# Gate and up of a feed-forward layer as a 2x2 block product: seven products for eight on a quarter of k

## The chip, the cores and the metric

The kernel runs on one core of one Trainium2 chip. The engines are TensorE (PE, with its weight loads as PEld), VectorE (DVE), ScalarE (ACT), GpSimd (POOL) and SyncE (SP, whose queue issues most DMA transfers). The metric is the device time in microseconds, as the median of several runs.

## The reference

One layer on 256 tokens of width 2048, all in float32. The part that the change touches is the feed-forward block, which stands in the layer twice, ahead of the mixer and behind it:

```
def swiglu(h, w_gate, w_up, w_down):
    return (jax.nn.silu(h @ w_gate) * (h @ w_up)) @ w_down

x = x + 0.5 * swiglu(rms_norm(x, ffn1_norm[i]), ffn1_w_gate[i], ffn1_w_up[i], ffn1_w_down[i])
```

`w_gate` and `w_up` are 2048 x 5632 and `w_down` is 5632 x 2048. Between the two feed-forward blocks stand an input projection, a state-space mixer with a GLU, a stick-breaking attention and an output projection; behind the second stands a gated per-layer embedding.

## The kernel before, in words

**Precision.** Every float32 operand of a large product is cut into a high part, rounded to the matmul's format (`hi`), and the rest (`lo`). A product of two such operands is made of three: hi·hi, lo·hi (activation lo, weight hi) and hi·lo. For weights, `split` (L165) does the cut: ScalarE casts `raw` to `whi` (L168), VectorE subtracts to make `wlo` (L171). `whi` and `wlo` have four buffers each, `raw` has three.

**Tiles.** k goes in tiles of 128, in quarters of 512 (one DMA of 1 MB on SP's queue, L274, one `raw`) and in halves of a quarter (2 k tiles, 128 x 1024 numbers, one split). A block of output columns is 512 wide, `NB`. The 256 tokens are two tiles `t` of 128. The activations are stationary, the weights stream: `gemm_half` (L277) sends for one half eight matmuls with `hi` weights (L284 and L285: activation hi, activation lo, for two k tiles and two t) and then four with `lo` weights (L289), into one PSUM bank for each t. `gemm_block` (L291) does this for all halves of k and calls `step()` after each.

**The layer's loop.** `ffn` (L379) is called twice: layer 1 with `bg=s5_prep` (the mixer's preparation runs beside it until block 6), layer 2 without. Each has 11 blocks of columns, `for f in range(NF)`: gate's block over 16 k tiles, its silu on ScalarE (L410), up's block over 16 k tiles, and the product of both on VectorE (L430), from PSUM:

```
hh[:, t * NB : (t + 1) * NB], in0=pu[t], scalar=xn.rs(t), in1=sg[...]
```

`turned` then turns the result on VectorE (L203, into `mid`) and through 16 small DMAs on SP's queue to `hT`, which the down projection cuts into `hhi` and `hlo` (`act`, L436) and multiplies by `w_down`.

**Buffers.** PSUM has four banks of 512 columns for products (`acc`). Activations in halves lie in the tags `nhi`/`nlo` (four buffers each) and `hhi`/`hlo` (two each). Layer 1's normalized input takes all of `n`, and `h` is free until the down projection; layer 2's (`kinds="hhnn"`) takes `h` and two of `n`.

**What sets the order.** The code traces instructions in the order in which it is written, with work put off by a number of steps: `put_off(n, fn)` runs `fn` at the (n+1)th `step()` from there, and a generator given to `start` advances one `yield` at each step. From the trace a list planner issues each engine's queue: it takes what its own costs say is ready, earlier code first, and only instructions in `pin(...)` keep their place. Each engine then works through its queue in that order and waits at semaphores.

Of the kernel before, what the change touches and what calls it, by code (L numbers as in the profile page):

```python
# [9 lines left out]
F32 = mybir.dt.float32  # L10
# [6 lines left out]
P = 128  # L17
# [16 lines left out]
def layer_kernel(ctx: ExitStack, tc: tile.TileContext, a: dict, shapes: dict, out: bass.AP):  # L34
# [45 lines left out]
    def acc(s="acc"):  # L80
        return accp.tile([P, NB], F32, tag="acc", name=uid(s))
# [83 lines left out]
    def split(hi, lo, src, scale=None, pinned=False):  # L165

        if scale is None:
            copy = nc.scalar.copy(hi, src)  # L168
            if pinned:
                pin(copy)  # L170
            nc.vector.tensor_tensor(out=lo, in0=src, in1=hi.bitcast(F32), op=ALU.subtract)  # L171
        else:
            split_each(hi.unsqueeze(1), lo.unsqueeze(1), src.unsqueeze(1), [scale])
# [103 lines left out]
    def gemm_half(ps, half, ts, start, stop, cols=slice(0, NB)):  # L277

        (ahi, alo), (h, hi, lo) = half
        for j in range(2):  # L280
            for t in ts:
                lh = ahi[:, 2 * h + j, t * P : (t + 1) * P]
                ll = alo[:, 2 * h + j, t * P : (t + 1) * P]
                nc.tensor.matmul(ps[t], lhsT=lh, rhs=hi[:, j, cols], start=start and j == 0, stop=False)  # L284
                nc.tensor.matmul(ps[t], lhsT=ll, rhs=hi[:, j, cols], start=False, stop=False)  # L285
        for j in range(2):
            for t in ts:
                lh = ahi[:, 2 * h + j, t * P : (t + 1) * P]
                nc.tensor.matmul(ps[t], lhsT=lh, rhs=lo[:, j, cols], start=False, stop=stop and j == 1)  # L289

    def gemm_block(act, w, n0, nkt, first=()):  # L291

        ps = [acc(), acc()]
        for k0 in range(0, nkt, 4):
            part = act(k0 // 4)
            quarter = first[k0 // 4] if k0 // 4 < len(first) else weight_halves(w, k0, min(4, nkt - k0), n0)
            for half in list(quarter):
                k = k0 + 2 * half[0]
                gemm_half(ps, (part, half), range(TT), k == 0, k + 2 == nkt)
                if first and half[0] == 0 and k0 + 4 < nkt:  # L300
                    act(k0 // 4 + 1)
                step()
        return ps
# [75 lines left out]
    def ffn(i, xn, nxt, bg=None):  # L379
        wg, wu, wd = (a[f"ffn{i}_w_{s}"][0] for s in ("gate", "up", "down"))  # L380
        hT = []
        pools = ExitStack()
        early = 6 if bg else NF
        hp = pools.enter_context(phase(f"h{i}"))
        side = ExitStack()
        prep = bg(side) if bg else None
        mids = {}

        def turned(hp, f, hh):
            pair, n_pair = f // 2, min(2, NF - f // 2 * 2) * 4  # L390
            if f % 2 == 0:
                mids[pair] = com("mid")[:, : 128 * TT * n_pair].rearrange(
                    "p (q t b f) -> p q t b f", q=4, t=TT, b=32
                )
            for t in range(TT):
                turn_blocks(mids[pair], hh[:, t * NB : (t + 1) * NB], t, f % 2 * 4, 4)
            if f % 2 or f == NF - 1:
                hf = get(hp, f"hT{pair}", T * n_pair)
                turn_quarters(hf.rearrange("p (t s f) -> p t s f", t=TT, f=n_pair), mids[pair], 8)
                hT.append(hf.rearrange("p (s f) -> p f s", f=n_pair))  # L400

        for f in range(NF):
            if prep and f == min(early, NF - 1):
                finish(prep)
                side.close()
                prep = None
                hp = pools.enter_context(phase(f"h{i}b"))
            def gate():
                for t in range(TT):
                    nc.scalar.activation(sg[:, t * NB : (t + 1) * NB], pg[t], AF.Silu, scale=xn.rs(t))  # L410

            first = ()
            if f == 0 and bg:
                warm_up(10)
                first = first_quarters(wg, xn)
            pg = gemm_block(xn, wg, f * NB, KD, first)
            sg = com("sg")
            if f == 0 and bg:
                for n in range(ND):
                    put_off(n, load_x, n)  # L420
                    put_off(n + 2, xn.squares, n)
                put_off(6, gate)
            else:
                gate()
            pu = gemm_block(xn, wu, f * NB, KD)
            if prep and f == 0:
                start(prep)
            hh = com("h")
            for t in range(TT):
                nc.vector.scalar_tensor_tensor(  # L430
                    out=hh[:, t * NB : (t + 1) * NB], in0=pu[t], scalar=xn.rs(t),
                    in1=sg[:, t * NB : (t + 1) * NB], op0=ALU.mult, op1=ALU.mult,
                )
            put_off(2, turned, hp, f, hh)

        def act(k):  # L436
            hi, lo = halves("h")
            split(hi, lo, hT[k // 2][:, k % 2 * 4 : k % 2 * 4 + 4, :])
            return hi, lo

        for n in range(ND):
            ps = gemm_block(act, wd, n * NB, F // P)
            for t in range(TT):
                nc.vector.scalar_tensor_tensor(
                    out=xt[t][n], in0=ps[t], scalar=0.5, in1=xt[t][n], op0=ALU.mult, op1=ALU.add
                )
            put_off(2, nxt.block, n)
        pools.close()
# [779 lines left out]
```

## Time and profile before

| | before |
|---|---|
| median of 3 runs | 1901.69 us (1900.64 to 1903.12) |
| span of the profiled execution, first to last instruction | 1898.3 us |
| what lies between that span and the median | 3.4 us |
| instructions | 23928 |
| matmuls on TensorE | 9142 |

The page lists for the profiled execution only its span; no other time of this one execution is given. "Busy" counts time in which an engine has an instruction running; matmuls overlap, so a matmul's mean duration (392 ns) is longer than the distance between two. "Idle before" in a group's row is the time that the engine stood still ahead of its instructions, with the instruction that ended the wait. In a timeline the columns are start and duration in us, engine, line, operation, output and input with their shapes, how many were merged, and the wait.

### The profile page before, as it was taken

To read this page: it belongs to the slowest core of one execution; us is meant where nothing else is said; L and a number is where in the kernel's file an instruction comes from. 1 tells how busy PE (TensorE), PEld (TensorE's weight loads), DVE (VectorE), ACT (ScalarE), POOL (GpSimd) and SP (SyncE) were. 2 spreads that over 40 slices of the span, in tenths; PEclk is the share of its full clock that TensorE was granted. 3 is DMA by queue.
4 is the path that set the end of the run, shared out by engine and by line. 5 is a ranking of instruction groups with operands and counts; after the bars stand their busy time and mean duration, and the time that the engine had idled before them with its cause. 6 is when DMAs were issued, how large, how long until landed. Compare 5 with 4: busy or idle time off the path is not lost.

```text
span 1898.3 us, 23928 instructions
## 1 busy us (share of the span) xinstructions
PE 1888.4 (99%) x9142; PEld 1563.8 (82%) x9142; DVE 1299.6 (68%) x1604; ACT 1105.7 (58%) x1217; POOL 30.6 (2%) x48
## 2 busy tenths in 40 slices
PE   9999999999999999999999999999999999999998
PEld 7888888888888888888898888888888888888886
DVE  8996765555688987686567655555555568898855
ACT  7466664444578886455785544444444457888754
POOL 0000000000000000010010000000000000000000
PEclk9999999999999999999999999999999999999999
DMA  8677877666656657776545656665656665666553
GB/s 323 225 243 260 261 247 236 197 209 209 215 185 209 209 190 277 235 243 205 172 156 172 222 187 217 200 210 191 220 189 216 201 223 188 205 209 209 196 200 122
DMA packets 225714, 402.55 MB, mean 212 GB/s; under 512 B 16704, under 2 KB 46656, under 8 KB 225472
## 3 DMA queue, kind: packets, MB, share of 16 engines
q1 hardware_dynamic: 212976, 385.99, 61.2%
q10 hardware_dynamic: 12624, 15.04, 2.3%
q8 instruction: 71, 1.16, 0.3%
q14 instruction: 43, 0.35, 0.1%
HBM read 369.53 MB, written 14.68 MB: 202 GB/s over the span
## 4 chain that ended last, share of the span: by engine, by line
PE 94%; DVE 2%; ACT 1%; issue 1%; DMA 1%; SPq 0%; DVEq 0%; ACTq 0%
PE acc L284 30%; PE acc L285 30%; PE acc L289 30%; DVE hlo L171 1%; ACT hhi L168 1%; DVE wlo L171 1%; DVE nlo L180 1%; PE aux L715 0%; PE acc L994 0%; PE acc L989 0%; PE acc L985 0%; PE aux L634 0%; DMA raw<-in_ffn_w_gate 0%; DMA h<-in_p_turned 0%; PE aux L767 0%
## 5 line engine op out<-in xcount | busy, mean ns | idle before, releaser
L171 DVE TENSOR_TENSOR wlo<-raw,whi 128x1024 fp32r<-128x1024 f32 x666 | 810.5, 1225 | 451.5 <-ACT whi L168 446.9
L168 ACT CAST whi<-raw 128x1024 fp32r<-128x1024 f32 x666 | 697.8, 1054 | 710.1 <-PE acc L285 658.4
L284 PE MATMUL acc<-whi,nhi 128*128 128x512 f32 x1568 | 614.2, 392 | 1.2 <-ACT whi L252 0.7
L285 PE MATMUL acc<-whi,nlo 128*128 128x512 f32 x1568 | 610.6, 389 | 0.0
L289 PE MATMUL acc<-wlo,nhi 128*128 128x512 f32 x1568 | 420.7, 389 | 0.0
L285 PE MATMUL acc<-whi,hlo 128*128 128x512 f32 x1056 | 411.6, 390 | 0.7
L284 PE MATMUL acc<-whi,hhi 128*128 128x512 f32 x1056 | 411.0, 389 | 0.0
L284 PEld LDWEIGHTS acc<-whi,nhi 128*128 128x128 f32 x1568 | 294.3, 188 | 64.9 <-ACT whi L252 1.8
L289 PEld LDWEIGHTS acc<-wlo,nhi 128*128 128x128 f32 x1568 | 294.2, 188 | 61.7 <-DVE wlo L171 0.2
L285 PEld LDWEIGHTS acc<-whi,nlo 128*128 128x128 f32 x1568 | 294.4, 188 | 60.0
L289 PE MATMUL acc<-wlo,hhi 128*128 128x512 f32 x1056 | 282.2, 389 | 0.0
L285 PEld LDWEIGHTS acc<-whi,hlo 128*128 128x128 f32 x1056 | 198.2, 188 | 44.7 <-DVE hlo L171 3.3
L289 PEld LDWEIGHTS acc<-wlo,hhi 128*128 128x128 f32 x1056 | 198.2, 188 | 41.2
L284 PEld LDWEIGHTS acc<-whi,hhi 128*128 128x128 f32 x1056 | 198.2, 188 | 40.7
L171 DVE TENSOR_TENSOR hlo<-hT,hhi 128x1024 fp32r<-128x1024 f32 x88 | 188.4, 2141 | 48.7 <-ACT hhi L168 48.7
L168 ACT CAST hhi<-hT 128x1024 fp32r<-128x1024 f32 x88 | 192.2, 2185 | 1.4 <-DMA raw<-in_ffn_w_gate 1.4
L203 DVE STREAM_TRANSPOSE mid<-h 128x512 f32<-128x512 f32 x44 | 47.0, 1156 | 0.0
L430 DVE SCALAR_TENSOR_TENSOR h<-acc,sm,sg 128x512 f32<-128x512 f32 x44 | 31.0, 745 | 19.4 <-PE acc L289 19.4
L410 ACT ACTIVATE sg<-acc,sm 128x512 f32<-128x512 f32 x44 | 27.7, 681 | 0.4 <-DVE sm L196 0.3
L178 ACT ACTIVATE nhi<-h,gains 128x256 fp32r<-128x256 f32 x40 | 24.0, 662 | 0.2 <-DVE h L1010 0.2
L180 DVE SCALAR_TENSOR_TENSOR nlo<-h,gains,nhi 128x256 fp32r<-128x256 f32 x40 | 23.1, 633 | 0.6 <-ACT nhi L178 0.6
L704 POOL COPY dec<-rho 128x512 f32<-128x512 f32 x8 | 10.6, 1348 | 729.0 <-DVE rt L741 564.5
(242 smaller groups left out, 762.7 us busy)
## 6 DMA issues: line engine op xcount, KB each, us to landing
raw<-in_ffn_w_up SPq DMA_DIRECT2D x88, 1024.0 KB, 5.5
raw<-in_ffn_w_down SPq DMA_DIRECT2D x88, 1024.0 KB, 5.0
raw<-in_ffn_w_gate SPq DMA_DIRECT2D x86, 1024.0 KB, 5.1
raw<-in_w_in SPq DMA_DIRECT2D x32, 1024.0 KB, 5.5
raw<-in_w_out SPq DMA_DIRECT2D x16, 1024.0 KB, 5.2
raw<-in_w_ple_gate SPq DMA_DIRECT2D x16, 1024.0 KB, 5.0
hT<-mid SPq DMA_DIRECT2D x160, 64.0 KB, 4.8
h<-mid SPq DMA_DIRECT2D x128, 32.0 KB, 3.7
```

Source lines behind the costliest of these rows:

```text
L168: copy = nc.scalar.copy(hi, src)
L171: nc.vector.tensor_tensor(out=lo, in0=src, in1=hi.bitcast(F32), op=ALU.subtract)
L178: nc.scalar.activation(hi[:, j, :], src[:, j, :], AF.Copy, scale=scale)
L180: nc.vector.scalar_tensor_tensor(out=lo[:, j, :], in0=src[:, j, :], scalar=scale, in1=hi[:, j, :].bitcast(F32), op0=ALU.mult, op1=ALU.subt ...
L203: nc.vector.transpose(mid[:, :, t, :, k0 : k0 + nk].rearrange("p q b f -> p f q b"), src.rearrange("p (f q b) -> p f q b", f=nk, q=4),)
L284: nc.tensor.matmul(ps[t], lhsT=lh, rhs=hi[:, j, cols], start=start and j == 0, stop=False)
L285: nc.tensor.matmul(ps[t], lhsT=ll, rhs=hi[:, j, cols], start=False, stop=False)
L289: nc.tensor.matmul(ps[t], lhsT=lh, rhs=lo[:, j, cols], start=False, stop=stop and j == 1)
L410: nc.scalar.activation(sg[:, t * NB : (t + 1) * NB], pg[t], AF.Silu, scale=xn.rs(t))
L430: nc.vector.scalar_tensor_tensor(out=hh[:, t * NB : (t + 1) * NB], in0=pu[t], scalar=xn.rs(t), in1=sg[:, t * NB : (t + 1) * NB], op0=ALU.m ...
L704: nc.gpsimd.tensor_copy(dvw[:, i], rho4[:, 8 * q : 8 * q + 8].unsqueeze(2).to_broadcast([P, 8, NC]))
```

## The change

In 14 of the 22 blocks of columns (layer 1: f = 7 to 10; layer 2: f = 1 to 10) the first quarter of k of gate and up is done together. With A the activations, cut into two token tiles (rows) and two halves of the quarter (columns), and B the weights, cut into two halves of k (rows) and gate and up (columns), A·B is a 2x2 product of blocks, and it is made of seven products of blocks, by Winograd's scheme, where it was eight. A product of blocks is 128 tokens by 256 of k by 512 columns: six matmuls (four with hi weights, two with lo). The other three quarters of k go on as before, into the same banks.

What each such block has in it:

- `fetch` loads the quarter of gate (`dg`) and of up (`du`), 1 MB each, for the next block, into tiles with one buffer each, and makes four sums of weights on VectorE (128 x 1024 each: `t1`, `t2`, `t3` in place of `b12`, `t4`). `t1`, `t2`, `t4` and `kept` take the free buffers of `h` (layer 1) or `n` (layer 2): `t1`, `t4` two of `hi`, `t2`, `kept` two of `lo`.
- `quarter_sums`, once for each layer, makes four sums of activation blocks and splits them.
- `pair` runs the seven products, each with a split of its own for its 128 x 1024 weights, made two products ahead. They go into three banks `x`, `a`, `y`; four of the sums are copied out by ScalarE on the way (`o6`, `o7` in `kept`, `o1`, `o5`). VectorE adds these copies to each other later (`sums`, three adds of 512), and at the end to the finished banks: `o1` to gate's second token tile ahead of its silu, `o6` and `o7` to both tiles of up. The last product `hh` then reads SBUF instead of PSUM.
- The steps: after products 1, 3, 5 and 6, and after each half of the other quarters, 16 in a block as before.

```diff
+    def product(ps, a, src, start):
+        (ahi, alo), hi, lo = a, *(wp.tile([P, 2, NB], F32R, tag=s, name=uid(s)) for s in ("whi", "wlo"))
+        split(hi, lo, src)
+        def run():
+            for j in range(2):
+                for i, l in enumerate((ahi, alo)):
+                    nc.tensor.matmul(
+                        ps, lhsT=l[:, j], rhs=hi[:, j], start=start and i + j == 0, stop=False, skip_group_check=True
+                    )
+            for j in range(2):
+                nc.tensor.matmul(ps, lhsT=ahi[:, j], rhs=lo[:, j], start=False, stop=j == 1, skip_group_check=True)
+        return run
...
+        def fetch(f, steps=6):
+            def g():
...
+                for d, w in ((dg, wg), (du, wu)):
+                    nc.sync.dma_start(d, w[:NB, f * NB : (f + 1) * NB].rearrange("(j p) n -> p j n", p=P))
+                b11, b21, b12, b22 = dg[:, :2], dg[:, 2:], du[:, :2], du[:, 2:]
...
+                for _ in range(steps):
+                    yield
+                for o, x, y in ((t1, b12, b11), (t2, b22, t1), (b12, b22, b12), (t4, b21, t2)):
+                    nc.vector.tensor_tensor(out=o, in0=x, in1=y, op=ALU.subtract)
+                    yield
...
+        def pair(f, prefetch):
+            (a11, a12, a22), (s1, s2, s3, s4) = left[0]
+            b11, b21, b22, t1, t2, t3, t4, kept = right.pop(f)
+            x, a, y = acc(), acc(), acc()
+            o6, o7 = kept[:, :NB], kept[:, NB:]
+            o1, o5 = get(hp, "o1", NB), get(hp, "o5", NB)
+            todo = [
+                (x, s2, t2, o6), (a, a11, b11, o1), (y, s1, t1, o5), (x, s3, t3, o7), (a, a12, b21, None),
+                (y, s4, b22, None), (x, a22, t4, None),
+            ]
+            runs = []
+            for i, (ps, l, r, o) in enumerate(todo):
+                while len(runs) < min(i + 3, len(todo)):
+                    n = len(runs)
+                    runs.append(product(*todo[n][:3], todo[n][3] is not None and n != 3))
+                runs[i]()
+                if o is not None:
+                    nc.scalar.copy(o, ps)
+                if i % 2 or i == 6:
+                    step()
+            if prefetch:
+                fetch(f + 1)
+            def sums():
+                nc.vector.tensor_tensor(out=o6, in0=o6, in1=o1, op=ALU.add)
+                nc.vector.tensor_tensor(out=o7, in0=o7, in1=o1, op=ALU.add)
+                nc.vector.tensor_tensor(out=o7, in0=o7, in1=o5, op=ALU.add)
+            put_off(3, sums)
+            rest([a, x], wg, f, ())
+            sg = com("sg")
+            nc.scalar.activation(sg[:, :NB], a, AF.Silu, scale=xn.rs(0))
+            nc.vector.tensor_tensor(out=sg[:, NB:], in0=x, in1=o1, op=ALU.add)
+            nc.scalar.activation(sg[:, NB:], sg[:, NB:], AF.Silu, scale=xn.rs(1))
+            z = acc()
+            rest([y, z], wu, f, (1,))
+            hh = com("h")
+            for ps, o in ((y, o6), (z, o7)):
+                nc.vector.tensor_tensor(out=o, in0=ps, in1=o, op=ALU.add)
+            for t, o in enumerate((o6, o7)):
...
+                    out=hh[:, sl], in0=o, scalar=xn.rs(t), in1=sg[:, sl], op0=ALU.mult, op1=ALU.mult
...
         for f in range(NF):
...
+            if f >= first_pair:
+                pair(f, f + 1 < NF)
+                continue
...
+            if f + 1 == first_pair:
+                left.append(quarter_sums(hp, xn(0)))
+                fetch(f + 1, 3)
             pu = gemm_block(xn, wu, f * NB, KD)
```

`rest` is `gemm_block` without the first quarter; `gemm_half` is given a set of token tiles that start afresh, so that `z` starts there and the other banks go on.

More of the change, by code (lines that the diff above doesn't have):

```diff
@@ L275, in weight_halves, with gemm_half @@
         return weight_split(raw, nk, own)
[L277 removed]
+    def gemm_half(ps, half, ts, start, stop, cols=slice(0, NB), **kw):
         (ahi, alo), (h, hi, lo) = half
+        starts = (ts if start else ()) if isinstance(start, bool) else start
         for j in range(2):
@@ L288, in gemm_half, with quarter_sums @@
                 lh = ahi[:, 2 * h + j, t * P : (t + 1) * P]
-                nc.tensor.matmul(ps[t], lhsT=lh, rhs=lo[:, j, cols], start=False, stop=stop and j == 1)
+                nc.tensor.matmul(ps[t], lhsT=lh, rhs=lo[:, j, cols], start=False, stop=stop and j == 1, **kw)
+    def product(ps, a, src, start):
[10 more added lines that the diff above has]
+        return run
+    def quarter_sums(pool, part):
+        hi, lo = part
+        full, s = (com("h").rearrange("p (j t) -> p j t", t=T), com("h").rearrange("p (i j t) -> p i j t", i=4, j=2))
+        nc.vector.tensor_tensor(out=full, in0=hi.bitcast(F32), in1=lo.bitcast(F32), op=ALU.add)
+        a11, a12, a21 = (full[:, 2 * k : 2 * k + 2, t * P : (t + 1) * P] for t, k in ((0, 0), (0, 1), (1, 0)))
+        a22 = full[:, 2:, P:]
+        for o, x, y, op in (
+            (0, a21, a22, ALU.add), (1, s[:, 0], a11, ALU.subtract), (2, a11, a21, ALU.subtract),
+            (3, a12, s[:, 1], ALU.subtract),
+        ):
+            nc.vector.tensor_tensor(out=s[:, o], in0=x, in1=y, op=op)
+        shi, slo = (pool.tile([P, 4, 2, P], F32R, name=uid(n)) for n in ("shi", "slo"))
+        split(shi, slo, s)
+        quarters = [
+            tuple(u[:, 2 * k : 2 * k + 2, t * P : (t + 1) * P] for u in part) for t, k in ((0, 0), (0, 1), (1, 1))
+        ]
+        return quarters, [(shi[:, i], slo[:, i]) for i in range(4)]
     def gemm_block(act, w, n0, nkt, first=()):
@@ new lines, in rest @@
+        def rest(ps, w, f, starts):
+            for k0 in range(4, KD, 4):
+                part = xn(k0 // 4)
+                for half in list(weight_halves(w, k0, 4, f * NB)):
+                    k = k0 + 2 * half[0]
+                    gemm_half(
+                        ps, (part, half), range(TT), starts if k == 4 else False, k + 2 == KD, skip_group_check=True
+                    )
+                    step()
[8 more added lines that the diff above has]
+                (y, s4, b22, None), (x, a22, t4, None),
+            ]
+            runs = []
[7 more added lines that the diff above has]
+                if i % 2 or i == 6:
+                    step()
+            if prefetch:
[16 more added lines that the diff above has]
+            for t, o in enumerate((o6, o7)):
+                sl = slice(t * NB, (t + 1) * NB)
+                nc.vector.scalar_tensor_tensor(
+                    out=hh[:, sl], in0=o, scalar=xn.rs(t), in1=sg[:, sl], op0=ALU.mult, op1=ALU.mult
+                )
+            put_off(2, turned, hp, f, hh)
```

17 lines of the change are left out of this document (15 added, 2 removed).

## The prediction

> **What bounds the kernel now.** I read the page's busy shares and chain first, then its costliest groups.
>
> ```profile
> span 1898.3 us, 23928 instructions
> PE 1888.4 (99%) x9142; PEld 1563.8 (82%) x9142; DVE 1299.6 (68%) x1604; ACT 1105.7 (58%) x1217; POOL 30.6 (2%) x48
> PE 94%; DVE 2%; ACT 1%; issue 1%; DMA 1%; SPq 0%; DVEq 0%; ACTq 0%
> L171 DVE TENSOR_TENSOR wlo<-raw,whi 128x1024 fp32r<-128x1024 f32 x666 | 810.5, 1225 | 451.5 <-ACT whi L168 446.9
> L168 ACT CAST whi<-raw 128x1024 fp32r<-128x1024 f32 x666 | 697.8, 1054 | 710.1 <-PE acc L285 658.4
> ```
>
> TensorE is busy 99% of the span and is 94% of the chain that ended last. ScalarE's cast mostly waits for a buffer that TensorE holds, VectorE's subtraction mostly for the cast: both run ahead and are held back by their four buffers. A matmul less on TensorE is therefore time gained, as long as the two stay ahead. Next the stretches of the stage that changes, as windows (time, then busy PE, PEld, DVE, ACT, POOL, the granted clock, DMA): one column block of the second feed-forward layer, all eleven but the first of them, and the down projection of the first layer.
>
> ```profile
> 1157.50:1201.00 43.50, 43.50 (x193) 36.02 (x192) 22.79 (x21) 18.05 (x18) 0.00 (x0) 1.00 0.70 217
> 1114.00:1550.00 436.00, 436.00 (x1925) 361.03 (x1924) 233.03 (x205) 184.39 (x182) 0.00 (x0) 1.00 0.64 205
> 543.50:716.00 172.50, 172.12 (x757) 141.50 (x756) 154.98 (x120) 141.40 (x120) 0.00 (x0) 1.00 0.59 200
> ```
>
> TensorE has no gap in ten blocks, at full clock. In the down projection VectorE is busy 154.98 of 172.5 us (90%) and ScalarE 82%, and TensorE still loses only 0.38 us: that is how full the helpers may be. Last, the timeline at the ends of blocks: VectorE's first and last product of gate and up in the second layer, then the seam at 1331 on all engines (the seam in order of time).
>
> ```profile
> 1113.31 1.41 DVE L430 SCALAR_TENSOR_TENSOR h<-acc,sm,sg 128x512 f32<-128x512 f32 x2 [1.09 <-PE acc L289]
> ...
> 1548.51 1.41 DVE L430 SCALAR_TENSOR_TENSOR h<-acc,sm,sg 128x512 f32<-128x512 f32 x2 [1.09 <-PE acc L289]
> ```
> ```profile
> 1328.59 1.23 DVE L171 TENSOR_TENSOR wlo<-raw,whi 128x1024 fp32r<-128x1024 f32 x1 [1.50 <-ACT whi L168]
> ...
> 1330.03 1.07 PE L289 MATMUL acc<-wlo,nhi 128*128 128x512 f32 x4
> 1330.22 1.05 ACT L168 CAST whi<-raw 128x1024 fp32r<-128x1024 f32 x1 [1.67 <-PE acc L285]
> ...
> 1330.91 1.41 DVE L430 SCALAR_TENSOR_TENSOR h<-acc,sm,sg 128x512 f32<-128x512 f32 x2 [1.09 <-PE acc L289]
> 1330.93 0.39 PE L284 MATMUL acc<-whi,hhi 128*128 128x512 f32 x1
> ...
> 1332.23 1.22 DVE L171 TENSOR_TENSOR wlo<-raw,whi 128x1024 fp32r<-128x1024 f32 x1
> ...
> 1333.36 2.16 DVE L203 STREAM_TRANSPOSE mid<-h 128x512 f32<-128x512 f32 x2
> ```
>
> From 1113.31 to 1548.51 are ten blocks: 43.52 us each, and with 192 matmuls in one, **226.7 ns a matmul**. A half (12 matmuls) takes 2.72 us, a product of the new kind (6) 1.36 us, of which its four with hi weights take 0.91. At the seam the cast at 1330.22 starts 0.19 us after the last hi matmuls; it fills the buffer of the half that just left and is the *fourth* half from there. So when block time 0 comes (1330.93), three halves lie ready.
>
> **The change part by part.** *Removed:* of the 48 matmuls on the first quarter of k, 42 are left. 14 blocks x 6 x 226.7 ns = **-19.04 us**. The new order sends all six matmuls of a product into one bank; the last resident block does that already, at the same pace:
>
> ```profile
> 1872.09 0.39 PE L284 MATMUL acc<-whi,nhi 128*128 128x512 f32 x1
> ...
> 1872.99 0.62 PE L289 MATMUL acc<-wlo,nhi 128*128 128x512 f32 x2
> 1873.44 0.39 PE L284 MATMUL acc<-whi,nhi 128*128 128x512 f32 x1
> ```
>
> Six in 1.35 us, so the new order costs nothing. [...]
>
> *Added to VectorE and ScalarE, per block.* Prices:
>
> ```profile
> 566.29 2.35 DVE L171 TENSOR_TENSOR wlo<-raw,whi 128x1024 fp32r<-128x1024 f32 x2
> L818 DVE TENSOR_TENSOR sg<-sg,sm 128x1024 f32<-128x1024 f32 x4 | 4.9, 1226 | 0.1
> L1083 DVE TENSOR_TENSOR e<-h,pg 128x512 f32<-128x512 f32 x7 | 4.5, 683 | 0.0
> L1081 DVE TENSOR_TENSOR h<-acc,sg 128x512 f32<-128x512 f32 x7 | 4.6, 687 | 9.6 <-PE acc L289 9.6
> L1105 DVE SCALAR_TENSOR_TENSOR x<-e,sm,x 128x512 f32<-128x512 f32 x7 | 4.8, 745 | 0.1
> L636 ACT COPY m<-aux 128x1024 f32<-128x1024 f32 x8 | 8.1, 1014 | 11.0 <-DMA scr_m1r<-m 8.8 <-PE aux L634 2.2
> L410 ACT ACTIVATE sg<-acc,sm 128x512 f32<-128x512 f32 x44 | 27.7, 681 | 0.4 <-DVE sm L196 0.3
> ```
>
> Two splits back to back take 2.35, so one costs VectorE 1.13 in a row; two 512-wide products take 1.41 (L430), so 0.66 each. VectorE gets three splits more and four sums of weights (7 x 1.13 = 7.9) and six 512-wide adds (6 x 0.66 = 4.0): 22.79 + 11.9 = 34.7 us of a block of 42.16, 82%. That is under the 90% at which the down projection feeds TensorE. ScalarE gets three casts and four copies out of PSUM, each between half of L636 and L410, say 0.6: 18.05 + 3.2 + 2.4 = 23.7 us, 56%. On average both are hidden behind TensorE. The sums of activations, once per layer (five VectorE operations, one split, under 5 us), and the first sums of weights lie in an ordinary block, where VectorE idles 1.5 us of each 2.72.
>
> *The burst* is what can cost. Seven splits in 9.5 us instead of four in 10.9, and right behind the seam. Time from the first product; products 3 to 6 (counting from 0) want their lo weights at 4.99, 6.35, 7.71, 9.07, the first half after them at 9.52 + 1.81 = 11.33; those of 0 to 2 lie ready. VectorE first closes the old block, four operations now instead of two (y+o6, z+o7 from PSUM, then two products): free at 2.64, the last result out at 2.73. Then the splits end at 3.9, 5.0, 6.1, 7.3, the two transposes (2.16) at 9.3, the next half's split at 10.5: every one 0.8 us early or more. ScalarE: the copy of product 0 into `kept` must wait until the old block's `kept` is free (2.73, since only two buffers are left for the pair t2/kept), and product 3 adds onto the same bank at 4.08, so it waits for that copy. If the copy is next on ScalarE it runs from 2.75 to 3.4; if product 5's cast (startable at 2.47, when product 1's hi matmuls are done) is ahead, from 3.4 to 4.1, some 0.2 us late with the hand-over. Both ends: 0 and 0.5 us per block; below 0 nothing, since no gap is there to close. I take 0.2, because the cast is startable earlier, **+2.8 us**. At the end of layer 1 `kept` also holds one of the down projection's two `lo` buffers until 2.73; that split (2.14 on hlo rows) is then out at some 4.9, wanted at 5.44: 0 to 1 us, I take **+0.3**.
>
> *Moved on SP's queue:* the first quarters (two loads of 1 MB) come behind the products into a single buffer that the splits free at about 7.3, so SP may stand there; the raws of gate's three other quarters are already in by then (three buffers), and the sums use them some 15 us later.
>
> ```profile
> raw<-in_ffn_w_gate SPq DMA_DIRECT2D x86, 1024.0 KB, 5.1
> raw<-in_ffn_w_up SPq DMA_DIRECT2D x88, 1024.0 KB, 5.5
> ```
>
> Two landings of 5.1 and 5.5 one after the other fit, bytes are the same: 0. Uncovered it would be 10.6 less the 8.2 us (three halves) that lie ready, 2.4 us per block.
>
> Sum: -19.04 + 2.8 + 0.3 = -15.9. On the span that is 1882.4; the median of the runs shown lies 3.4 us above the span, which I keep: 1901.7 - 15.9 = **1885.8 us**.
>
> **The rivals.** *A: stalls inside the products take a part.* If the transposes come ahead of product 4's split (before, they follow one split after the product, 1333.36), that split ends at 7.0 instead of 5.0, wanted at 6.35: 0.65 us; with the copy's 0.2 some 0.85 a block, 12 us: 1901.7 - 19.0 + 12 = 1894.7. For it: the order at the seam. Against: the fourth split wasn't startable there, and here it is.
>
> *B: ScalarE's queue keeps the order of the code, and the gain is gone.* There product 3's cast stands behind the copy that waits until 2.73: cast 3.4 to 4.5, lo out at 5.7 for 4.99 (0.7 late), and each later one is copy 0.6 + cast 1.0 against 1.36, some 0.25 late each, three times: 1.4 us a block, 20 us, about 1902. [...] What decides is the order in which the program issues them, and on that the trace has two lines of ScalarE:
>
> ```profile
> 1308.46 1.05 ACT L168 CAST whi<-raw 128x1024 fp32r<-128x1024 f32 x1 [1.67 <-PE acc L285]
> 1309.42 1.26 ACT L410 ACTIVATE sg<-acc,sm 128x512 f32<-128x512 f32 x2
> ```
>
> The cast at 1308.46 belongs to up's fourth half and stands in the code behind the silu; it is issued ahead of it. So casts do pass waiting work.
>
> *C, slower: VectorE's queue closes the old block before it splits for the new one,* as the code has it. Then product 0's lo comes at 2.64 + 1.23 = 3.9, wanted at 0.91: 3.0 us a block, 42 us, 1924. With only one split ahead of the closing the next is late by 1.6 (3.87 for 2.27), 22 us, 1905; with two, 0.24. It decides from fewer than two splits ahead on. Against it: three are ahead now. For it: the closing is twice as long and the splits ahead now need sums that are made in the same queue.
>
> **How the numbers follow.** Forecast (0 to 0.5 us a block; 1882.7 to 1890) 0.62; A (to 1897) 0.17; B 0.08; C 0.11; 0.02 for anything else. The low end is -19.04 with no stall, less 1 us for the spread of the runs. The range 1881.5 to 1898 takes in the forecast and A. A difference of 0.2% (3.8 us) is about what this measurement can tell from none: faster 0.78, same 0.09, slower 0.13.
>
> **What would show it.** After: 9058 matmuls (84 fewer), blocks of 42.2 to 42.7 us between VectorE's closing products; VectorE near 34.7 us in each; idle time of TensorE only ahead of the products' lo matmuls or product 3, with the copies on ScalarE as releaser. Blocks over 43.5 us, or weight loads waiting for wlo in sum over 10 us, would make it wrong; gaps right at the seam mean C, casts behind copies mean B, transposes ahead of product 4's split mean A.

## The result, and the profile after

The changed kernel takes 1886.26 us (median of four runs, 1885.17 to 1887.87), the kernel before beside it 1901.16 (1900.09 to 1903.12): ratio 0.9916, 95% interval 0.9904 to 0.9929. The forecast was 1885.8. The page of the profiled execution (1886.81 us, span 1885.0): its span, the busy shares, the chain that ended last, and two groups.

```profile
span 1885.0 us, 24143 instructions
PE 1874.1 (99%) x9058; PEld 1548.1 (82%) x9058; DVE 1460.9 (78%) x1798; ACT 1174.7 (62%) x1317; POOL 32.5 (2%) x48
PE 86%; DVE 3%; issue 2%; ACT 1%; DMA 1%; SPq 0%; DVEq 0%; ACTq 0%
L300 PE MATMUL acc<-whi,shi 128*128 128x512 f32 x112 | 44.5, 397 | 0.0
L285 PE MATMUL acc<-whi,hhi 128*128 128x512 f32 x896 | 348.8, 389 | 0.0
```

9058 matmuls, 84 fewer, and TensorE is still busy 99% of the span. (Lines have moved: the products are L300 with hi weights and L304 with lo, the ordinary halves L285, L286 and L290, the copies L494, the closing adds and products L515 and L518.) One thing to keep in mind: a hi matmul on `shi` lasts 397 ns (the products' other groups 391 to 395), an ordinary one on `hhi` 389.

The length of a block, from VectorE's closing adds at the end of the second layer's first pair block and of its last, and the ten pair blocks of that layer as a window (busy PE, PEld, DVE, ACT, POOL, clock, DMA):

```profile
1153.46 1.29 DVE L515 TENSOR_TENSOR t<-acc,t 128x512 f32<-128x512 f32 x2 [1.09 <-PE acc L290]
...
1535.06 1.29 DVE L515 TENSOR_TENSOR t<-acc,t 128x512 f32<-128x512 f32 x2 [1.09 <-PE acc L290]
```
```profile
1111.06:1535.06 424.00, 424.00 (x1861) 349.25 (x1860) 336.46 (x327) 232.34 (x253) 0.00 (x0) 1.00 0.64 208
```

(1535.06 - 1153.46) / 9 = **42.40 us**, where it was 43.52: 1.12 us a block, 15.7 in fourteen. TensorE has no gap, at a granted clock of 1.00; VectorE is busy 33.65 us of a block (79%), ScalarE 23.23. But 186 matmuls at 226.7 ns are 42.16 us, so each block is 0.24 us longer than its matmuls account for, although nothing waits. The seam and the products in the timeline; the rows are a selection, in order of time:

```profile
1195.86 1.29 DVE L515 TENSOR_TENSOR t<-acc,t 128x512 f32<-128x512 f32 x2 [1.09 <-PE acc L290]
1195.88 0.40 PE L300 MATMUL acc<-whi,shi 128*128 128x512 f32 x1
1197.07 1.41 DVE L518 SCALAR_TENSOR_TENSOR h<-t,sm,sg 128x512 f32<-128x512 f32 x2
1197.28 0.39 PE L300 MATMUL acc<-whi,hhi 128*128 128x512 f32 x1
1197.97 0.58 ACT L494 COPY t<-acc 128x512 f32<-128x512 f32 x1
1198.39 1.22 DVE L171 TENSOR_TENSOR wlo<-du,whi 128x1024 fp32r<-128x1024 f32 x1
1198.67 0.39 PE L300 MATMUL acc<-whi,shi 128*128 128x512 f32 x1
1200.07 0.40 PE L300 MATMUL acc<-whi,shi 128*128 128x512 f32 x1
1200.77 0.37 SPq L450 DMA_DIRECT2D dg<-in_ffn_w_gate  x1
1201.79 1.22 DVE L171 TENSOR_TENSOR wlo<-t,whi 128x1024 fp32r<-128x1024 f32 x1
1202.93 2.31 DVE L203 STREAM_TRANSPOSE mid<-h 128x512 f32<-128x512 f32 x2
1205.65 0.39 PE L285 MATMUL acc<-whi,hhi 128*128 128x512 f32 x1
```

VectorE closes the old block, makes four splits and only then transposes. ScalarE's copy of product 0 into `kept` (1197.97) is done 1.5 us before product 3 starts (1200.07). No instruction in the products is late. Yet the 42 matmuls from 1195.88 to 1205.65 take 232.4 ns each, at a granted clock of 1.00, and the ordinary ones behind them 226.7 again. 42 x 5.7 ns = 0.24 us: that is all of the difference. It isn't only the four products on `shi` and `slo`, at some 233 ns: product 1, on ordinary activations (1197.28 to 1198.67), takes 231.5 ns a matmul, and products 4 and 6 take 231.3 and 231.5.

Where the span's 13.3 us come from: four pair blocks in layer 1 gave 4.5 and ten in layer 2 gave 11.2; the stretch ahead of the pairs lost 1.9, between the layers 0.4, the end 0.15. The stretch ahead runs the same code in both kernels, but for `quarter_sums` and the first `fetch` in its last block, and that block takes 45.67 us in both. Its end is VectorE's last ordinary product in layer 1, at 325.89 in the trace of before; in two executions of the changed kernel (the second from the experiments below):

```profile
327.77 1.41 DVE L558 SCALAR_TENSOR_TENSOR h<-acc,sm,sg 128x512 f32<-128x512 f32 x2 [1.09 <-PE acc L290]
```
```profile
330.25 1.41 DVE L558 SCALAR_TENSOR_TENSOR h<-acc,sm,sg 128x512 f32<-128x512 f32 x2 [1.09 <-PE acc L290]
```

2.5 us apart in one and the same kernel; over all traces here, the slower staggered kernel's (333.0) apart, the point lies between 325.7 and 331.4. From there to the end the two executions agree within 0.1 us (1557.2). So the 1.9 us are within what this stretch varies by from one execution to the next, and the 2.4 us between the spans of these two come from there. Counted from that point on, the change takes the kernel from 1572.4 to 1557.2 us: 15.2 us.

### The profile page after: what moved, and what is told of

It reads as the page before. It is cut to its first block, busy times and chain, and to the rows that moved or that the text cites. A ratio compares the mean times of both kernels' runs of the same rounds, so it can differ in the third digit from the quotient of the medians.

```text
span 1885.0 us, 24143 instructions
## 1 busy us (share of the span) xinstructions
PE 1874.1 (99%) x9058; PEld 1548.1 (82%) x9058; DVE 1460.9 (78%) x1798; ACT 1174.7 (62%) x1317; POOL 32.5 (2%) x48
## 4 chain that ended last, share of the span: by engine, by line
PE 86%; DVE 3%; issue 2%; ACT 1%; DMA 1%; SPq 0%; DVEq 0%; ACTq 0%
PE acc L285 25%; PE acc L286 25%; PE acc L290 25%; PE acc L300 5%; PE acc L304 2%; DVE wlo L171 1%; DVE hlo L171 1%; ACT hhi L168 1%; DVE nlo L180 1%; DMA ceq<-in_ssm_c_laid 1%; PE aux L843 0%; PE acc L1122 0%; PE acc L1117 0%; PE acc L1113 0%; PE aux L762 0%
## 5 line engine op out<-in xcount | busy, mean ns | idle before, releaser
L168 ACT CAST whi<-raw 128x1024 fp32r<-128x1024 f32 x610 | 638.5, 1054 | 523.8 <-PE acc L286 429.7
L171 DVE TENSOR_TENSOR wlo<-raw,whi 128x1024 fp32r<-128x1024 f32 x610 | 737.9, 1226 | 206.2 <-ACT whi L168 201.9
L285 PE MATMUL acc<-whi,nhi 128*128 128x512 f32 x1504 | 589.4, 392 | 1.4 <-ACT whi L252 1.0
L286 PE MATMUL acc<-whi,nlo 128*128 128x512 f32 x1504 | 585.8, 390 | 0.0
L290 PE MATMUL acc<-wlo,nhi 128*128 128x512 f32 x1504 | 403.8, 389 | 0.8 <-DVE wlo L171 0.8
L286 PE MATMUL acc<-whi,hlo 128*128 128x512 f32 x896 | 349.5, 390 | 0.7
L285 PE MATMUL acc<-whi,hhi 128*128 128x512 f32 x896 | 348.8, 389 | 0.0
L285 PEld LDWEIGHTS acc<-whi,nhi 128*128 128x128 f32 x1504 | 282.4, 188 | 62.9 <-ACT whi L252 1.8
L290 PEld LDWEIGHTS acc<-wlo,nhi 128*128 128x128 f32 x1504 | 282.2, 188 | 60.6 <-DVE wlo L171 1.7
L286 PEld LDWEIGHTS acc<-whi,nlo 128*128 128x128 f32 x1504 | 282.5, 188 | 57.8 <-DVE nlo L253 0.3
L290 PE MATMUL acc<-wlo,hhi 128*128 128x512 f32 x896 | 239.5, 389 | 0.0
L286 PEld LDWEIGHTS acc<-whi,hlo 128*128 128x128 f32 x896 | 168.2, 188 | 39.0 <-DVE hlo L171 3.7
L290 PEld LDWEIGHTS acc<-wlo,hhi 128*128 128x128 f32 x896 | 168.2, 188 | 34.9
L285 PEld LDWEIGHTS acc<-whi,hhi 128*128 128x128 f32 x896 | 168.2, 188 | 34.5
L171 DVE TENSOR_TENSOR wlo<-t,whi 128x1024 fp32r<-128x1024 f32 x42 | 51.4, 1223 | 41.8 <-ACT whi L168 41.8
L168 ACT CAST whi<-t 128x1024 fp32r<-128x1024 f32 x42 | 44.2, 1053 | 46.8 <-PE acc L286 46.8
L171 DVE TENSOR_TENSOR wlo<-dg,whi 128x1024 fp32r<-128x1024 f32 x28 | 34.2, 1223 | 20.2 <-ACT whi L168 20.2
L300 PE MATMUL acc<-whi,shi 128*128 128x512 f32 x112 | 44.5, 397 | 0.0
```

What stands on the lines that cost most here:

```text
L285: nc.tensor.matmul(ps[t], lhsT=lh, rhs=hi[:, j, cols], start=t in starts and j == 0, stop=False, **kw)
L300: nc.tensor.matmul(ps, lhsT=l[:, j], rhs=hi[:, j], start=start and i + j == 0, stop=False, skip_group_check=True)
```

## The experiments

Two questions: is the order of the helpers' queues, which the rivals B and C were about, what carries the gain, and what makes the products' matmuls 5.7 ns longer? In the measured times, "before" is the kernel before, run on the same chip.

**Six matmuls in a row into one bank, without the change.** In `gemm_half` of the kernel before:

```diff
-        for j in range(2):
-            for t in ts:
+        for t in ts:
+            for j in range(2):
                 ... # hi weights: activation hi, activation lo
-        for j in range(2):
-            for t in ts:
+            for j in range(2):
                 ... # lo weights
```

> The kernel before, with its own arithmetic, and the order of the new products everywhere in gate, up, down and the projections: six matmuls of a half into one bank (four with hi weights, two with lo), then six into the other. In the profile of the changed kernel the 42 matmuls of the products follow each other at 232.4 ns, the others at 226.7, and that makes 0.24 us a block. If the order (six into one bank, lo weights wanted after four) is the cause, all 7,872 wide matmuls slow by 5.7 ns: some 45 us slower than before, 1946 us. If not, the time is the one before, 1901 us, and the wide matmuls stay at 226.7 ns.

1910.84 us (1909.57 to 1913.49), ratio 1.0044 (1.0027 to 1.006). The pace is untouched: blocks of gate and up stay at 43.52 us. So the order is not what costs 5.7 ns, and for gate and up the prediction's "the new order costs nothing" holds. The 7.5 us come from elsewhere. From TensorE's list of waits in this kernel (who waits for whom, us in total, times, longest):

```profile
PE acc L285 <- DVE hlo L171: 5.6, 12, 0.6
```

The kernel before has no such wait among its matmuls. The down projection splits its activations as it goes, and the new order finds `hlo` late twelve times. The list counts a wait from the end of the matmul before it; without a wait the next one would have started 0.16 us earlier (389 ns long, 226.7 apart). So an estimate of the loss is 5.6 + 12 x 0.16 = 7.5 us, all of it.

**Copies that read SBUF.** ScalarE's four copies take a tile of x in place of the PSUM bank, so their values, and the output, are not the layer's.

```diff
-                    nc.scalar.copy(o, ps)
+                    nc.scalar.copy(o, xt[0][0])
```

> The changed kernel; ScalarE's four copies in each product block read a tile in SBUF instead of the PSUM bank (the sums o1, o5, o6, o7 then hold other numbers, and the output is not the layer's). ScalarE's load stays; TensorE no longer has to wait before products 3 to 6 for a bank that ScalarE still reads. If those waits, or the reading of PSUM beside the matmuls, slow the products, the pace in them goes to 226.7 ns, a block to 42.16 us, the whole to 1883 us. If not, the blocks stay at 42.40 us and the time at 1886 us.

1887.18 us, ratio 0.992 (0.9902 to 0.9938); blocks of 42.40 us, as in the changed kernel. ScalarE's reads of the banks are not the cause.

**ScalarE in the order of the code (rival B).**

```diff
-                    nc.scalar.copy(o, ps)
+                    pin(nc.scalar.copy(o, ps))
...
-        split(hi, lo, src)
+        split(hi, lo, src, pinned=True)
```

> The changed kernel with the casts and copies of the products kept on ScalarE's queue in the order of the code: product 3's cast stands behind the copy of product 0, and so on (the planner put one more cast ahead of each copy). Rival B prices this at 1.4 us a block, 20 us: 1906 us, the gain gone. If the copy does not wait for the old block to close (in the changed kernel's trace it starts 2.1 us after the first product and not at 2.75), the loop of copy 0.58, cast 1.05 and subtraction 1.23 just fits and it costs under 0.3 us a block: 1886 to 1890 us.

1895.15 us (1893.08 to 1898.55), ratio 0.9961 (0.9949 to 0.9973). ScalarE, VectorE's closing adds, and VectorE and TensorE where the block loses its time (a selection, in order of time):

```profile
1198.43 0.59 ACT L494 COPY t<-acc 128x512 f32<-128x512 f32 x1 [3.97 <-PE acc L304]
1198.92 1.05 ACT L168 CAST whi<-du 128x1024 fp32r<-128x1024 f32 x1
```
```profile
1196.81 1.29 DVE L515 TENSOR_TENSOR t<-acc,t 128x512 f32<-128x512 f32 x2 [1.09 <-PE acc L290]
1239.90 1.29 DVE L515 TENSOR_TENSOR t<-acc,t 128x512 f32<-128x512 f32 x2 [1.09 <-PE acc L290]
```
```profile
1199.34 1.24 DVE L203 STREAM_TRANSPOSE mid<-h 128x512 f32<-128x512 f32 x1
1200.41 1.22 DVE L171 TENSOR_TENSOR wlo<-du,whi 128x1024 fp32r<-128x1024 f32 x1
1201.56 1.19 DVE L203 STREAM_TRANSPOSE mid<-h 128x512 f32<-128x512 f32 x1
1202.60 1.20 DVE L171 TENSOR_TENSOR wlo<-dg,whi 128x1024 fp32r<-128x1024 f32 x1
1203.86 0.73 PE L304 MATMUL acc<-wlo,hhi 128*128 128x512 f32 x2 [0.35 <-DVE wlo L171]
```

The copy waits 3.97 us for product 0 with the cast for product 3 behind it: that is the order of B. Blocks are 43.09 us: 0.69 us a block are lost, half of the 1.4 that B was priced at. But the loss isn't where B put it. The block starts at 1196.84; the copy runs 1.6 us into it and not at 2.73, and product 3's lo weights are out at 4.8 us, in time for the 4.99 of the working. TensorE waits at one place in a block, ahead of product 4's lo matmuls (0.35 us), because VectorE now turns one token tile of the old block ahead of product 3's split and the other ahead of product 4's. That split ends 7.0 us into the block, and product 4 takes 2.01 us where it took 1.39: nearly all of the loss, and the stall that rival A priced, with the split at 7.0 and 0.65 us lost.

**VectorE in the order of the code (rival C).**

```diff
-        split(hi, lo, src)
+        nc.scalar.copy(hi, src)
+        pin(nc.vector.tensor_tensor(out=lo, in0=src, in1=hi.bitcast(F32), op=ALU.subtract))
```

> The changed kernel with the products' subtractions kept on VectorE's queue in the order of the code, so that the closing of the old block (four operations) stands ahead of the first product's lo weights. Rival C prices this at 3.0 us a block, 42 us: 1928 us. If something else bridges the seam the time stays at 1886 us.

1918.25 us (1915.09 to 1921.48), ratio 1.0081 (1.0062 to 1.01): slower than before.

```profile
1207.40 1.29 DVE L516 TENSOR_TENSOR t<-acc,t 128x512 f32<-128x512 f32 x2 [7.68 <-PE acc L290]
1208.60 1.41 DVE L519 SCALAR_TENSOR_TENSOR h<-t,sm,sg 128x512 f32<-128x512 f32 x2
1209.92 1.22 DVE L296 TENSOR_TENSOR wlo<-t,whi 128x1024 fp32r<-128x1024 f32 x1
...
1252.16 1.29 DVE L516 TENSOR_TENSOR t<-acc,t 128x512 f32<-128x512 f32 x2 [9.20 <-PE acc L290]
```

VectorE stands 7.68 us ahead of the closing with nothing it may do, and the first `wlo` is out 3.7 us after the block's start, as priced (3.9). A block is 44.76 us, 2.36 more. It is less than C's 3.0: in this trace the hi matmuls of products 1 and 2 run ahead of product 0's lo matmuls, and TensorE waits 0.83 us ahead of these, 0.40 ahead of product 1's and 0.20 ahead of the lo matmuls of the first half behind the products.

**The weight sums made twice, and three times.** One loop in `fetch`, with 2 or 3:

```diff
-                    nc.vector.tensor_tensor(out=o, in0=x, in1=y, op=ALU.subtract)
+                    for _ in range(3):
+                        nc.vector.tensor_tensor(out=o, in0=x, in1=y, op=ALU.subtract)
```

> The changed kernel with each of the four weight sums of a block made twice, so VectorE has 4.9 us more per block, 39.6 of 42.4 us (93%). The third sum is written over one of its inputs, so doing it twice changes its value and the result is not the layer's. Theory (the sums are hidden and VectorE's slack is used by nothing): blocks stay at 42.4 us, the time within 0.2% of 1886.3. Rival (VectorE's queue is already tight, and a longer one delays the splits): blocks of 43 us and more, 1895 us or more.

> The changed kernel with each of the four weight sums made three times. VectorE is busy 33.77 us of a block of 42.40 in the changed kernel and 38.07 with the sums made twice, where the block stayed at 42.40; with three it comes to about 42.4, the whole block. Theory (VectorE's slack is used by nothing until it runs out): the bound is now VectorE, and what it must still wait for TensorE (1.09 us ahead of its first closing add in every block) comes on top: blocks of 42.4 to 43.6 us, 1886 to 1903 us. Rival (the splits are late long before VectorE is full): blocks of 44.5 us and more, 1915 us or more.

1885.26 us (ratio 0.9901, 0.9886 to 0.9917) and 1888.34 us (0.9928, 0.9912 to 0.9945). One block of each as a window, the sums made twice first:

```profile
1194.70:1237.10 42.40, 42.40 (x187) 34.92 (x186) 38.17 (x37) 22.74 (x26) 0.00 (x0) 1.00 0.60 199
```
```profile
1194.34:1236.74 42.40, 42.40 (x187) 34.94 (x186) 42.37 (x42) 22.73 (x26) 0.00 (x0) 1.00 0.60 200
```

With VectorE busy 42.37 of 42.40 us the block is still 42.40 us long. The change's sums are hidden, and nearly 9 us a block were left. (In that trace splits back to back, 1.22 us long, start 1.14 us apart on VectorE, so 42.37 us busy is not yet more work than fits; the wait of 1.09 us ahead of the closing add is gone in that kernel.)

**What sets the 232.4 ns.** Before's own trace has two more kinds of slow stretch, which the prediction left out: the last projection, on `pT`, and four halves of the last resident block, just ahead of the rows that the prediction quoted for "six in 1.35 us". Where each begins and ends:

```profile
1811.87 0.40 PE L284 MATMUL acc<-whi,pT 128*128 128x512 f32 x1
1814.67 0.39 PE L284 MATMUL acc<-whi,nhi 128*128 128x512 f32 x1
1863.84 0.40 PE L284 MATMUL acc<-whi,nhi 128*128 128x512 f32 x1
1869.35 0.39 PE L284 MATMUL acc<-whi,nhi 128*128 128x512 f32 x1
1870.72 0.39 PE L284 MATMUL acc<-whi,nhi 128*128 128x512 f32 x1
1874.80 0.39 PE L284 MATMUL acc<-whi,pT 128*128 128x512 f32 x1
```

Twelve matmuls on `pT` in 2.80 us are 233 ns each. 24 on `nhi` from 1863.84 to 1869.35 are 229.6 ns, 18 of the same form from 1870.72 to 1874.80 are 226.7, both at a granted clock of 1.00. (The resident block sends six matmuls for each half, on `nhi` and `nlo`.) `pT`, `shi` and `slo` have one thing in common in the program's layout of SBUF: they lie above byte 151200 of each partition, all other stationary operands of wide matmuls below 128672. Two kernels with other layouts: one with `shi`, `slo` and `pT` laid low (x's tiles move up for it, and the mixer's `ua` shares the place), beside it the changed kernel itself, and one with the activations of the kernel before moved up.

```diff
+    lowp = ctx.enter_context(tc.tile_pool(name="low", bufs=1)) # ahead of the weights
...
-        shi, slo = (pool.tile([P, 4, 2, P], F32R, name=uid(n)) for n in ("shi", "slo"))
+        shi, slo = (
+            lowp.tile([P, 1024], F32R, tag=f"low{i}", name=uid(n)).rearrange("p (i j t) -> p i j t", i=4, j=2)
+            for i, n in enumerate(("shi", "slo"))
+        )
```
```diff
-    actp = ctx.enter_context(tc.tile_pool(name="act", bufs=1))
     comp = ctx.enter_context(tc.tile_pool(name="com", bufs=1))
+    actp = ctx.enter_context(tc.tile_pool(name="act", bufs=1))
```

> The changed kernel with another layout of SBUF and nothing else. The stationary operands of four of the seven products (shi, slo) lie at bytes 151520 to 159712 and 176096 to 184288 of each partition, those of the last projection (pT) at 151520 to 155616; all other stationary operands of wide matmuls lie below byte 128672, and in the traces of before and after it is the products and pT alone that run 12 or more matmuls on end at 232 ns. Here shi, slo and pT lie at 5792 to 13984. Theory (the place of the stationary operand sets the pace): the 42 matmuls of the products at 226.7 ns, blocks of 42.15 to 42.2 us, pT's halves at 226.7, the whole 3.2 to 3.8 us below the changed kernel (about 1882.7). Rival (one split per six matmuls, or the busier helpers, set the pace): 232.4 ns and blocks of 42.40 as before, time as the changed kernel.

> The changed kernel itself beside the one with the other layout, on the same chip: 1886.3 us, between 1885.2 and 1887.9.

> The kernel before, with the scratch tiles (com) laid ahead of the activations (act), so that the activations move up by 22.5 KB: hhi and hlo then lie at 134816 to 151200, the fourth buffer of nlo at 130720 to 134816, nhi and the other nlo still below 130720. No instruction is changed. Theory (place of the stationary operand): the matmuls on hhi and hlo go at 232.4 ns: 4224 of the two down projections and 2112 of the second layer's gate and up, 6336 x 5.7 = 36 us, and up to 15 us more for those around the one nlo buffer: 1937 to 1953 us. Rival: no matmul changes, 1901 us.

Laid low: 1884.26 us (1882.26 to 1886.16), ratio 0.9893 (0.9876 to 0.991), the changed kernel beside it 1889.24 (1888.83 to 1890.22), ratio 0.992 (0.9905 to 0.9935). That is above the 1885.2 to 1887.9 expected of the changed kernel, in every run; its trace has the difference in the stretch ahead of the pairs, which ends at 330.25 there. The closing adds and the products' matmuls with the sums laid low:

```profile
1154.78 1.29 DVE L519 TENSOR_TENSOR t<-acc,t 128x512 f32<-128x512 f32 x2 [1.09 <-PE acc L291]
1196.94 1.29 DVE L519 TENSOR_TENSOR t<-acc,t 128x512 f32<-128x512 f32 x2 [1.09 <-PE acc L291]
```
```profile
L301 PE MATMUL acc<-whi,shi 128*128 128x512 f32 x112 | 43.6, 389 | 0.0
```

Blocks of exactly 42.16 us and 389 ns: no instruction was changed, only places. But moving `hhi` and `hlo` up to bytes 134816 to 151200 did nothing: 1903.62 us, ratio 0.9997 (0.9986 to 1.0009), the matmuls on `hhi` still 389 ns. "High is slow" could now hold only above byte 151200, and the kernel with all at 480 below, where `shi` keeps its place, ends that too. What else differs in the layouts is where a tile begins, counted here within 512 bytes. The small tiles, 320 bytes, lie between the activations and the tiles behind them, so `shi`, `slo` and `pT` begin 480 bytes behind a multiple of 512, and the weights and activations 160; that also fits the resident block, whose slow halves have weights at 480 and activations at 160. Three more layouts:

```diff
+    smp = ctx.enter_context(tc.tile_pool(name="small", bufs=10)) # 11 for "all at 0"
     wp = ctx.enter_context(tc.tile_pool(name="wts", bufs=4))
...
-    smp = ctx.enter_context(tc.tile_pool(name="small", bufs=10))
```
```diff
-            actp.tile([P, 4, T], F32R, tag=kind + s, name=uid(kind + s), bufs={"n": 4, "h": 2}[kind])
+            actp.tile([P, 4 * T + 8], F32R, tag=kind + s, ...)[:, : 4 * T].rearrange("p (k t) -> p k t", t=T)
```

> The changed kernel with the small tiles moved ahead of the weights, a buffer more of them, and the output that nobody reads of the squares in bf16 (1 KB less), so that every tile of weights and activations, shi, slo and pT among them, begins at a multiple of 512 bytes of its partition. In the changed kernel whi and wlo begin 160 bytes behind a multiple of 512, as do nhi, nlo, hhi and hlo (all fast: 226.7 ns), while shi, slo and pT begin 480 behind one (slow: 232.4 ns). The layout with shi, slo and pT at 160 gave 226.7 ns throughout and blocks of 42.16 us, and moving hhi and hlo up to bytes 134816 to 151200, still at 160, changed nothing. Theory 1 (stationary and moving operand must begin at the same offset): all at 226.7 ns, blocks of 42.16 us, about 1882 to 1884 us. Theory 2 (480 behind a multiple is bad, whatever the moving operand): the same here. Theory 3 (tiles above byte 151200 are bad): 232.4 ns in the products, blocks of 42.40, as the changed kernel. If offset 0 is better than 160, the pace falls below 226.7 ns and the whole by up to some per cent.

> The changed kernel with the small tiles (320 bytes) moved ahead of the weights, so that weights and activations all begin 480 bytes behind a multiple of 512, as shi, slo and pT do already; these stay where they are. Theory 1 (equal offsets of the two operands): all at 226.7 ns, products too, blocks of 42.16 us, about 1882 to 1884 us. Theory 2 (480 is bad by itself): every wide matmul at 232.4 ns, some 8300 x 5.7 = 47 us more, about 1930 us. Theory 3 (place above byte 151200): products at 232.4, the rest at 226.7, 1886 us.

> The changed kernel with 32 bytes between one activation tile and the next (and the squares' unread output in bf16 to make room), so that nhi's four buffers begin 160, 192, 224 and 256 bytes behind a multiple of 512, nlo's 288 to 384, hhi's 416 and 448, hlo's 480 and 0, shi, slo and pT 352, and whi and wlo stay at 160. Theory 1 (equal offsets): only the halves on nhi at 160 at 226.7 ns, the others slower in a way that depends on the distance, 1900 to 1935 us. Theory 2 (an offset of its own, seen modulo 128): only those with remainder 96 (224, 352, 480) slow. Theory 3 (place): only shi, slo and pT slow, 1886 us.

| begin behind a multiple of 512 | weights | activations | shi, slo | block | median, us | ratio to before |
|---|---|---|---|---|---|---|
| changed kernel | 160 | 160 | 480 | 42.40 | 1889.24 | 0.992 |
| sums laid low | 160 | 160 | 160 | 42.16 | 1884.26 | 0.9893 |
| all at 480 | 480 | 480 | 480 | 42.16 | 1883.26 (1880.77 to 1886.29) | 0.989 (0.9868 to 0.9911) |
| all at 0 | 0 | 0 | 0 | 42.16 | 1881.08 (1880.61 to 1886.29) | 0.9884 (0.9862 to 0.9906) |
| activations staggered by 32 | 160 | 0 to 480 | 352 | 43.11 | 1919.37 (one run) | |

The first two rows come from one chip and the last three from another, so compare the ratios. The row of the products and that of `pT` in the kernel with all at 480, and two rows of the staggered one:

```profile
L300 PE MATMUL acc<-whi,shi 128*128 128x512 f32 x112 | 43.6, 389 | 0.0
L285 PE MATMUL acc<-whi,pT 128*128 128x512 f32 x14 | 5.4, 389 | 0.0
```
```profile
L287 PE MATMUL acc<-whi,nhi 128*128 128x512 f32 x1504 | 596.5, 397 | 1.3 <-ACT whi L254 0.8 <-ACT whi L170 0.5
L287 PE MATMUL acc<-whi,hhi 128*128 128x512 f32 x896 | 352.0, 393 | 0.0
```

`shi` at 480 was slow beside weights at 160 (397 ns a matmul) and is fast beside weights at 480 (389 ns), at the same bytes: in these layouts not its own place but where the two operands begin relative to each other decides. With the resident block, whose weights lie at 480 beside activations at 160 (229.6 ns start to start in the trace of before), all four pairings of 160 and 480 have been measured, and the two unequal ones are slow. The two groups of hi matmuls on `pT`, 18 of two widths in each, last 365 ns in the mean with all at 0 and all at 480 and 366 with the sums laid low, 372 and 369 in the changed kernel.

The pairing of a single matmul does not explain everything. In the trace of before the six matmuls on `nhi` right behind `pT` (1814.67 on) take 231.7 ns, the six after them 226.7, and this fits products 1, 4 and 6 (231.3 to 231.5 ns), six matmuls each and each right behind a product on `shi` and `slo`. The six on `pT` in the resident block (1874.80 on), with weights at 480 as well, take 230.5 right behind a fast stretch (226.7). Why six, isn't shown.

Where the activations are staggered, the block is 43.11 us = 186 x 231.8 ns. That halves on the `nhi` buffer at 160 go at 226.7 ns, as theory 1 expected, isn't shown: the row of `nhi` puts its four buffers together, at 397 ns a matmul (392 in the changed kernel). There `nhi` and `nlo` also alternate with different offsets, so quickly that single differences cannot be told apart. Which differences are good remains open: 0 was fast (226.7 ns), 320 slow both ways round (some 233 and 229.6). That 512 is the period isn't shown either, nor is the mechanism in the chip.

The medians of the three layouts with equal offsets lie below the changed kernel's, but the intervals of their ratios overlap, so the three can't be told apart, and the lowest, 1881.08 us, is not shown to be the best. Part of any such lead is the stretch ahead of the pairs. From VectorE's product that ends that stretch on, the traces take 1557.2 us (changed), 1553.9 (sums low), 1553.2 (all at 0) and 1553.0 (all at 480): 3.3 to 4.2 us for equal offsets, where 14 x 0.24 plus some 0.3 on `pT`, 3.7 in all, were expected.

## Why the prediction was right, and where it was not

*Removed matmuls*, -19.04: as said, 84 fewer, and TensorE without a gap.

*"Six in 1.35 us, so the new order costs nothing"*: this is the step that failed, mis-sized by +0.24 us a block, 3.4 us in all. In gate and up the order does cost nothing; the pace of the new matmuls was taken from a stretch whose operands begin at equal offsets, and `shi` and `slo` don't begin where the weights do. The layouts settle this.

*The copy's wait, +2.8*: it didn't occur, and TensorE has no idle time in the pair blocks of layer 2, where the prediction looked for it ahead of product 3 and the lo matmuls. The copy ran at 2.09 us of block time and not at 2.75, straight behind product 4's cast and ahead of product 5's: by then only the first of the two products of L518, the one that reads `o6`, is over (1.19 + 0.74 = 1.93), and the working had made it wait for both. Product 3, expected at 4.08, began at 4.19. So +2.8 for a stall that isn't there stands against +3.4 for a pace that wasn't seen. That the two are of one size is luck: the number came out right with the wrong cause.

*End of layer 1, +0.3*: the stretch between the layers is 0.36 us longer. The size agrees; that it is the held `lo` buffer was not tried.

*VectorE and ScalarE*, 34.7 and 23.7 us a block: measured 33.65 and 23.23. Hidden, and with far more room than "under 90%" claimed. The block is 42.40 us long whether VectorE is busy 33.65 us of it or, with the sums made three times, 42.37.

*The burst*: splits forecast to end at 3.9, 5.0, 6.1 and 7.3 ended at 3.7, 4.9, 6.0 and 7.1; the transposes at 9.4 (9.3), the next half's split at 10.4 (10.5). This part of the working holds in every figure.

*SP's queue*: `dg` is issued 4.9 us into the block, and TensorE has no gap behind it.

*The span*: -19.04 + 3.36 + 0.36 + 0.15 + 1.88 (the stretch ahead) = -13.3, against -15.9 forecast; without the stretch ahead, which varies by as much from one execution to the next, -15.2. The medians fell by 14.9 us (1901.16 to 1886.26). They hide the span's difference in part: the 3.4 us that were kept between span and median were 1.8 us around the span (1886.81 - 1885.0) plus 1.6 by which that execution of before lay under the median.

*The rivals*: A did not happen in the changed kernel, where the transposes come behind the fourth split. The orders of B and C were kept off by the planner: with the code's order they take 0.69 and 2.36 us a block, and C makes the kernel slower than before. B's price was too high because it had the copy wait until 2.73 and product 3 late, and neither happened; what the block loses under B's order is A's stall. C's price took TensorE's order as fixed, and in the trace it changed.

## What to carry to other kernels

When work on the engine that bounds is replaced by less work there, ask of the new work not only how much it is but at what pace it goes, and take the pace from rows that have the same operands in the same places. A gain of this kind hangs on the order in which the helpers' queues are issued, so look at that order before counting their shares. And compare stretches of a trace that repeat (a block, or a fixed point to the end) rather than whole runs: 0.24 us a block shows plainly there and is lost in the spread of the medians.

## What the runs showed of the hardware

In these traces wide matmuls (128x128 by 128x512) go at 226.7 ns or at some 229 to 233 ns start to start, at a granted clock of 1.00 and with the weight load at 188 ns in both. What set the slow ones apart in the layouts tried is where their operands begin in SBUF. Offsets within 512 bytes that are equal for the stationary and the moving operand were fast: all at 0, all at 480 and the products at 160 (sums laid low) gave blocks of 42.16 us, 186 x 226.7 ns. 480 against 160 was slow whichever of the two was which, 233 ns with the stationary operand at 480 (`pT` in the trace of before, and the products on `shi` and `slo` in the changed kernel), 229.6 with the moving one there (the resident block in the trace of before). Six matmuls behind a change of operands were slow as well, 231.7 ns on `nhi` behind `pT`. Why, isn't shown. The offsets alone made up to 2.8% of pace (233 against 226.7).
